# A decoder layer on one core: group 0's banded keys and values projected from unmodulated tokens, the adaLN shift added as a bias

## The chip, the cores and the metric

The kernel runs on one core of a Trainium2 chip. The metric is device time in microseconds (us) of one execution; the median over several executions counts. The engines of the core are TensorE (PE, with its weight loads listed as PEld), VectorE (DVE), ScalarE (ACT), GpSimd (POOL) and SyncE (SP). Each engine executes its own list of instructions strictly in that list's order; between engines, semaphores say when a tile is ready or free again.

## The reference, cut to what matters

One layer for S = 2048 tokens of width D = 1024. It begins with

```python
mod = silu(c) @ w_ada + b_ada                 # w_ada: 1024 x 3072
shift, scale, gate = split(mod, 3)
h = rms_norm(x, g_pre) * (1.0 + scale) + shift
proj = h @ w_in
qa, ka, va, fa, za, qb, kb, vb, zb = split(proj)
oa = forgetting_attention(qa, ka, va, fa + b_fgate) * silu(za)
ob = sliding_window_sink_attention(rope(qb), rope(kb), vb) * silu(zb)
y = concat(oa, ob) @ w_out
x = x + gate * rms_norm(y, g_post)
```

What the change touches is the way from x, `scale` and `shift` to h, and from h to `kb` (the keys of the sliding-window branch, 128 columns), `vb` (its values, 128 columns) and `fa` (the logits of the forget gates, 8 columns).

Written per column d of x, with xn the normalised x, G[d] = g_pre[d](1 + scale[d]), and shift[d]: h = xn G + shift, so h @ W = xn @ (G W) + shift @ W. The kernel before takes the left side for every token. The kernel after takes the right side for the first 512 tokens of kb, vb and fa.

## The kernel before, in words

**Groups and units.** The tokens stand in four groups of 512 (`ci` 0 to 3), each of four tiles `xt` of 128 tokens; the 1024 columns stand in eight slices of 128 (`KT`, index k). `hT[ci]` holds h transposed (columns on the partitions), as a high and a low float16 part. A weight is scaled by a power of two, made into a high part (`w_high`, ACT) and a low part (`w_low`, DVE), and a product is three float16 matmuls per slice: high x high, low x high, high x low. A unit of `kb` is one slice (three matmuls of 128x512), a unit of `vb` is four slices for 128 tokens (twelve matmuls of 128x136, values and forget gates together). `zb0` is a quarter of the weights of the banded branch's gate; its units look like those of `kb`.

**The start block.** It runs before the first unit and is written out by hand, engine by engine:

1. `c` is turned to columns, silu is taken. The positions are spread over 128 partitions by a matmul, and DVE makes the rotary angles from them (multiplied, reduced by 2 pi in six steps, clipped: tiles `ang`, `kh`, `kl`), ACT the sines.
2. The adaLN product: half 1 of `w_ada` is `scale`, half 0 is `shift`. Each half is eight tiles `wa` of 512 KB. Some are multiplied on PE (`ada_pe`, four float32 matmuls of 128x512 each), some are multiplied by silu(c) and added up on DVE (`ada_dve`, into `acc`), and `ada_sum` adds `acc` with a matmul against ones. `ada_col` picks the column form out of the sum (eight small DVE instructions).
3. Group 0: `squares` (ACT, a sum of squares per token tile), `root` (1/sqrt of the mean by a shift of the bits and three Newton steps, twelve instructions of 128x4: on DVE for group 0, on POOL for the others), `normal` (x times that root).
4. `pH`, a power of two that bounds h, and the factors `Gp` and `Shp` (G and shift, scaled by 2^14 / pH).
5. `turn`: four PE transposes per slice, then ACT applies `Gp` and `Shp` (Identity with scale and bias; the high part directly, the float32 `hf` beside it) and DVE takes the low part.

Group 1's squares, root and the normalisation of two of its tiles stand in this block too.

**The units and their slices.** After the start block a list `punits` runs in order: per group `kb` (8 units), `vb` (8 units), then some others; for group 0 that is `zb0` group 0 (8 units). Between them stand the transposes of the next group (`turn_x`, four of 128x128 per slice k, then ACT and DVE as in `turn`) at the places of the table `at_`. `at_slice(n, f)` puts an action at unit n (squares, root and normal of group ci + 2 in this manner), and `after(n, f)` puts the evacuation of a result one or more units behind the unit. The order on each engine is fixed by this program text; nothing is rearranged at run time.

**Queues.** SP's queue loads x and `w_ada`: x tiles 0 and 1 behind the scale half, x tiles 2 and 3 between tiles 1 and 2 of the shift half, x tiles 4 to 7 behind that. A transfer on it starts only when the one eight places ahead has landed. POOL's queue loads the weights of `kb`, `vb`.

**The end.** The output stage takes its own 1/sqrt with the same bit shift and Newton steps (`rsqrt_parts`, DVE), between the last product and the last store.

## Time and profile before

| | |
|---|---|
| median of 3 runs | 1151.11 us (1150.71 to 1152.66) |
| profiled execution: span from first to last instruction | 1149.5 us |
| profiled execution: mean granted TensorE clock | 0.995 of full |
| PE busy | 1117.5 us, 97% of the span |
| DVE, ACT, POOL busy | 930.4, 660.2, 211.1 us |
| DMA moved | 119.84 MB, mean 104 GB/s |

The span of the profiled execution lies 1.6 us below the median of the runs. "Busy" is the time in which an engine executed; matmuls are pipelined, so a busy PE is one that has a matmul under way, not one at its peak. The stretch that the change touches is the first 125 us and the last 10 us of the span.

### The profile page before, as it was taken

To read this page: it belongs to the slowest core of one execution; us is meant where nothing else is said; L and a number is where in the kernel's file an instruction comes from. 1 tells how busy PE (TensorE), PEld (TensorE's weight loads), DVE (VectorE), ACT (ScalarE), POOL (GpSimd) and SP (SyncE) were. 2 spreads that over 40 slices of the span, in tenths; PEclk is the share of its full clock that TensorE was granted. 3 is DMA by queue.
4 is the path that set the end of the run, shared out by engine and by line. 5 is a ranking of instruction groups with operands and counts; after the bars stand their busy time and mean duration, and the time that the engine had idled before them with its cause. 6 is when DMAs were issued, how large, how long until landed. Compare 5 with 4: busy or idle time off the path is not lost. (4 is left out here: it accounts for less than half of the span.)

```text
span 1149.5 us, 25258 instructions
## 1 busy us (share of the span) xinstructions
PE 1117.5 (97%) x9854; PEld 653.9 (57%) x9854; DVE 930.4 (81%) x2149; ACT 660.2 (57%) x1148; POOL 211.1 (18%) x328
## 2 busy tenths in 40 slices
PE   7899999999999999999999999999999999999997
PEld 3466545667755855555555555555555555544444
DVE  7878468968988568889888899888888888778885
ACT  3776245655555412676767667666776778634332
POOL 1222135645566420010010110001000000000000
PEclk8999999999999999999999999999999999999999
DMA  9934254423232232443244342213311336687643
GB/s 338 347 96 88 74 100 80 101 60 93 58 85 84 55 94 52 82 102 29 79 65 88 83 72 70 37 48 78 44 43 34 85 96 216 142 222 202 199 138 110
DMA packets 123134, 119.84 MB, mean 104 GB/s; under 512 B 64729, under 2 KB 100610, under 8 KB 123014
## 3 DMA queue, kind: packets, MB, share of 16 engines
q1 hardware_dynamic: 112046, 85.69, 27.3%
q0 software_dynamic: 10816, 32.50, 13.3%
q8 instruction: 77, 1.26, 0.6%
q14 instruction: 43, 0.35, 0.1%
q10 hardware_dynamic: 152, 0.04, 0.0%
HBM read 64.49 MB, written 25.18 MB: 78 GB/s over the span
## 5 line engine op out<-in xcount | busy, mean ns | idle before, releaser
L1367 ACT ACTIVATE p<-sta,lift,scl_qk 128x1024 f32<-128x1024 f32 (+2 forms) x160 | 171.9, 1075 | 131.0 <-PE sta L1361 82.0
L353 PE MATMUL bk<-hT,wh_qk 128*128 128x512 f16 x768 | 194.7, 378 | 0.0
L1374 DVE TENSOR_TENSOR pha<-p,pha 128x1024 f16<-128x1024 f32 (+2 forms) x160 | 169.1, 1057 | 0.2 <-ACT pha L1371 0.2
L1314 DVE TENSOR_REDUCE a_m<-bk 128x1 f32<-128x512 f32 x192 | 130.4, 686 | 45.5 <-PE bk L1311 44.5
L1589 PE MATMUL bk<-wohl,oz 128*128 128x512 f16 x744 | 163.7, 379 | 1.1 <-DVE oz L1538 0.7
L1371 ACT ACTIVATE pha<-p 128x1024 f16<-128x1024 f32 (+2 forms) x160 | 148.1, 926 | 5.9 <-PE poa L1387 1.2
L1589 PEld LDWEIGHTS <-oz 128*128 128x128 f16 x744 | 70.6, 98 | 84.6 <-DVE oz L1538 1.8
L1387 PE MATMUL poa<-vt,pha 128*128 128x65 f16 x1088 | 116.1, 192 | 1.4 <-DVE pha L1374 1.4
L1384 PE MATMUL poa<-vt,pha 128*128 128x65 f16 x1088 | 116.6, 193 | 0.8 <-DVE ona L1393 0.7
L1386 PE MATMUL poa<-vt,pha 128*128 128x64 f16 x1088 | 116.6, 194 | 0.0
L353 PEld LDWEIGHTS <-wh_qk 128*128 128x128 f16 x768 | 72.1, 97 | 74.5 <-issue 2.1
L1360 PE MATMUL sta<-T 128*128 128x512 f16 (+1 forms) x320 | 110.9, 346 | 2.9 <-ACT p L1367 2.8
L1311 PE MATMUL bk<-T 66*128 66x512 f16 (+2 forms) x320 | 109.7, 348 | 2.8 <-DVE a_m L1314 1.9
L1384 PEld LDWEIGHTS <-pha 128*128 128x128 f16 x1088 | 101.5, 96 | 15.5 <-DVE ona L1393 1.9
L1361 PE MATMUL sta<-T 69*128 69x512 f16 (+1 forms) x320 | 109.8, 348 | 0.0
L1386 PEld LDWEIGHTS <-pha 128*128 128x128 f16 x1088 | 100.9, 97 | 11.4
L1387 PEld LDWEIGHTS <-pha 128*128 128x128 f16 x1088 | 100.8, 99 | 1.8 <-DVE pha L1374 1.8
L353 PE MATMUL bk<-hT,wh_za 128*128 128x512 f16 x384 | 99.7, 378 | 0.0
L353 PE MATMUL bk<-hT,wh_zb 128*128 128x512 f16 x384 | 92.1, 379 | 0.5 <-ACT wh_zb L271 0.3
L371 PE MATMUL bk<-wh_va,hT 128*128 128x256 f16 x768 | 91.9, 273 | 0.0
L353 PE MATMUL bk<-hT,wh_qb 128*128 128x512 f16 x384 | 91.2, 379 | 0.0
L371 PEld LDWEIGHTS <-hT 128*128 128x128 f16 x768 | 73.3, 98 | 12.2 <-issue 2.1
(459 smaller groups left out, 1919.0 us busy)
## 6 DMA issues: line engine op xcount, KB each, us to landing
hT<-in_x_dram SPq DMA_DIRECT2D x20, 512.0 KB
wa<-in_w_ada_dram SPq DMA_DIRECT2D x16, 512.0 KB
z_d<-tz POOLq DMA_DIRECT2D x32, 256.0 KB, 2.9
T<-z_d SPq DMA_DIRECT2D x16, 512.0 KB
T<-stq SPq DMA_DIRECT2D x62, 128.0 KB
out_dram<-hT SPq DMA_DIRECT2D x15, 512.0 KB
xt<-in_x_dram SPq DMA_DIRECT2D x12, 512.0 KB
qs<-qf SPq DMA_DIRECT2D x80, 64.0 KB
```

Of the source, the lines that this page charges most:

```text
L353: PE.matmul(ps, whl[:, a, k, :], hT[ci][:, b, k, :], start=(k == 0 and n == 0), stop=(k == KT - 1 and n == 2))
L371: PE.matmul(ps[:, (u % 2) * 2 * P:(u % 2 + 1) * 2 * P], hT[ci][:, a, k, u * P:(u + 1) * P], wv[p][:, b, k, :], start=(k == 0 and n == 0), ...
L1314: V.tensor_reduce(m3[:, u, pc:pc + 1], mx[:, :w], axis=AX.X, op=ALU.max)
L1360: PE.matmul(self.st[:, o:o + w], T[:, 3, kb_], T[:, 1, qc], start=True, stop=False)
L1361: PE.matmul(self.st[:, o:o + w], T[0:XR, 2, kb_], T[0:XR, 0, qc], start=False, stop=not diag)
L1367: A.activation(self.p32[:, :self.w], self.st[:, :self.w], AF.Exp, scale=scl[f"qk{self.hd}"][:], bias=lift[:])
L1371: A.activation(self.ph[:, 0, :self.w], self.p32[:, :self.w], AF.Copy)
L1374: V.tensor_tensor(self.ph[:, 1, :self.w], self.p32[:, :self.w], self.ph[:, 0, :self.w], op=ALU.subtract)
L1384: PE.matmul(po[:, u, :], ph[:, 0, pq], vt[:, b, hd, 0:65], start=(self.first and n == 0 and u == 0), stop=False)
L1386: PE.matmul(po[:, u, 0:64], ph[:, 0, pq], vt[:, b, hd, 65:VW], start=False, stop=False)
L1387: PE.matmul(po[:, u, :], ph[:, 1, pq], vt[:, b, hd, 0:65], start=False, stop=(self.last and n == len(self.blocks) - 1))
L1589: PE.matmul(py, self.hl[:, i, k, :], w_slot(8 * j + k)[:, cc], start=(k == 0 and m_ == 0), stop=(k == KT - 1 and m_ == 2))
```

## The change

**Order of the start.** All four x tiles of group 0 are loaded between the two halves of `w_ada`. The `wa` tiles lie in the memory of `hT[1]` and `hT[2]`, which are not yet in use, so there are eight of them, each used for one tile of each half. On DVE the angles are split in parts and stand behind the copy of the columns `cols` and between the `ada_dve` steps of the scale half. Bounds are taken from maxima (`mx5`, `top`) with one transposition instead of a second matmul for the bound of h.

**Group 0.** x is only normalised, then transposed (`turn_plain`: ACT copies the high part, DVE subtracts the low one). The weights of `kb`, `vb`, `fa` are multiplied per row by `Gs` (G times a power of two) and split (`w2_high` 16 on ACT, `w2_low` 16 on DVE). The units of `kb` and `vb` for group 0 stand in the start block, among the matmuls of the shift half (`ada_pe` for tiles 0 to 2, `ada_dve` for tiles 3 to 7). Then comes `shift`: `ada_sum(0)` stands in the middle of the `vb` units, and the factors `Gp`, `Shp`, `Gx` behind it. shift @ W is made with small matmuls (`pb`; for `vb` from `shb`, `Shp` spread along the free axis by two POOL copies of 128x1024) and added when the results are evacuated (`bkb`, `bvb`).

**The plain weights.** For groups 1 to 3 `w_scale`, `w_high` and `w_low` of `kb` and `vb` are made as before, behind the factors of the shift half.

**Groups 1 and 2.** Squares, root and normal of group 1 stand behind that. Group 0's place in `punits` is sixteen empty units; group 1's transposes stand in a row between them. Squares, root and normal of group 2 stand among the units of group 1, not of group 0; those of group 3 remain there.

**Later modulation.** `remake(k)` modulates `hT[0]` slice by slice among group 1's units (two ACT and two DVE instructions of 128x512 for each of eight slices). The units of `zb0` for group 0 move to the list of `ci == 2`.

**1/sqrt.** All of them become a power of -0.5 on POOL, two instructions for a group, and in the output stage two POOL instructions and one on DVE. `gacc` takes a factor 32 in an instruction that was there.

The diff, cut to its core:

```diff
+    def remake(k):
+        hg = hst.tile([P, CH], F32, tag="hf", name="hg")
+        hi, lo = hT[0][:, 0, k, :], hT[0][:, 1, k, :]
+        A.activation(hg[:], lo, AF.Identity, scale=Gx[:, k:k + 1], bias=Shp[:, k:k + 1])
+        def high():
+            V.scalar_tensor_tensor(hg[:], hi, Gx[:, k:k + 1], hg[:], op0=ALU.mult, op1=ALU.add)
+            A.activation(hi, hg[:], AF.Copy)
+        after(1, high)
+        after(2, lambda: V.tensor_tensor(lo, hg[:], hi, op=ALU.subtract))
...
     def root(ci):
         ss, rst = rstd[ci]
-        rsqrt_mean(rst, ss[:], 4, G if ci else None)
+        f = 1.0 if ci else 2.0 ** -18
+        rv = sm(4, "rs_v")
+        G.tensor_scalar(rv[:], ss[:], f / D, f * EPS, op0=ALU.mult, op1=ALU.add)
+        G.tensor_tensor(rst[:], rv[:], mhalf[:].broadcast_to([P, 4]), op=ALU.pow)
...
         for k in (1, 3, 5, 7):
             ada_pe(1, k)
-        for k in (2, 4, 6):
-            ada_dve(1, k, k == 2)
-        for k in range(2):
-            load_ada(0, k)
-        for t in range(2, 4):
-            load_x(t)
-        for k in range(2, KT):
+        angle_a()
+        ada_dve(1, 2, True)
...
+        ada_dve(1, 6, False)
+        ada_sum(1, True)
...
+        ada_pe(0, 0, True)
+        turn_plain(0)
+        turn_plain(1)
+        ada_pe(0, 1)
+        for k in range(2, KT):
+            turn_plain(k)
+            ku[k - 2]()
+            if k == 4:
+                ada_pe(0, 2)
+                ada_dve(0, 3, True)
+            if k == 6:
+                ada_dve(0, 4, False)
+        for k in range(KT):
+            w2_high(k, P, VB)
+            w2_low(k, P, VB)
+            if k == 1:
+                ada_dve(0, 5, False)
+            if k == 5:
+                ada_dve(0, 6, False)
+        ku[6]()
+        ku[7]()
+        ada_dve(0, KT - 1, False, 2)
+        for n, u in enumerate(vu):
+            if n == 4:
+                ada_sum(0, True)
+            u()
...
+        w_scale("kb")
+        w_high("kb")
+        w_low("kb", 0, 1)
+        w_scale("vb")
+        w_high("vb")
+        w_low("vb", 0, 1)
...
+        squares(1)
+        root(1)
...
-        add("kb", kb_units(ci))
-        add("vb", vb_units(ci))
+        if ci == 0:
+            punits += [lambda: None for _ in range(16)]
+        else:
+            add("kb", kb_units(ci))
+            add("vb", vb_units(ci))
         if ci < 3:
-            add(*others[ci])
+            if ci:
+                add(*others[ci])
             if ci == 2:
+                add(*others[0])
...
+                for k in range(KT):
+                    at_slice(n0 + 20 + 3 * k, lambda k=k: remake(k))
...
-                    for _ in rsqrt_parts(self.rst, self.ss[:, 2:3], 1, self.more):
-                        pass
+                    V.tensor_tensor(self.more, self.ss[:, 2:3], self.more, op=ALU.add)
+                    G.tensor_tensor(self.rst[:], self.more, mhalf[:], op=ALU.pow)
```

Three places where the order of an engine moves. A row is: line, operation, output, inputs, shape, and how many alike stand in a row.

The first is DVE in the scale half, before (`ang`, `kh`, `kl` are the angles; `cols` is the copy of the columns that a PE transposition made; `acc1` collects the scale half, `wr_kv` holds the weights of `kb` and `vb`, whose maxima are taken):

```order
L583 SCALAR_TENSOR_TENSOR ang_222<-kl_224,ang_222 128x512
L585 TENSOR_SCALAR ang_222<-ang_222 128x512
L590 SCALAR_TENSOR_TENSOR kh_223<-ang_222 128x512
L591 TENSOR_SCALAR kh_223<-kh_223 128x512
L596 COPY cols_192<-bk2_138 128x32
L537 TENSOR_SCALAR acc1_207<-wa12_163,sil_126 128x1024
L539 SCALAR_TENSOR_TENSOR acc1_207<-wa14_167,sil_126,acc1_207 128x1024
L539 SCALAR_TENSOR_TENSOR acc1_207<-wa16_171,sil_126,acc1_207 128x1024
L619 TENSOR_REDUCE mx3_288<-wr_kv_183 128x1 x2
```

The same place after:

```order
L633 MEMSET zero_213 128x128
L644 COPY cols_194<-bk2_143 128x32
L648 TENSOR_REDUCE mx5_227<-cols_194 128x1 x3
L667 TENSOR_SCALAR ang_231<-bk1_142,colc_193 128x512
L668 TENSOR_SCALAR kl_233<-ang_231 128x512
L669 TENSOR_SCALAR kl_233<-kl_233 128x512
L670 TENSOR_SCALAR kh_232<-kl_233 128x512
L671 TENSOR_SCALAR kh_232<-kh_232 128x512
L672 TENSOR_TENSOR kl_233<-kl_233,kh_232 128x512
L612 TENSOR_SCALAR acc1_209<-hT1_108,sil_132 128x1024
L676 SCALAR_TENSOR_TENSOR ang_231<-kh_232,ang_231 128x512
```

The copy of `cols` stood behind all angles, and stands now ahead of the first. The multiplications into `acc1`, which stood behind the angles in a row, are now spread between them.

The second is ACT around the squares of group 1 (`junk`, with `hT3` as the memory of group 1's x tiles), before:

```order
L271 ACTIVATE wh_vb_343<-wr_kv_183,w_sw_338 128x1088
L433 ACTIVATE xt0_175<-xt0_175,rst_295 128x1024
L433 ACTIVATE xt1_177<-xt1_177,rst_295 128x1024
L433 ACTIVATE xt2_264<-xt2_264,rst_295 128x1024
L433 ACTIVATE xt3_266<-xt3_266,rst_295 128x1024
L421 ACTIVATE junk_409,ss_407<-hT3_110 128x1024
L421 ACTIVATE junk_411,ss_407<-hT3_110 128x1024
L421 ACTIVATE junk_413,ss_407<-hT3_110 128x1024
L447 ACTIVATE hT0_107<-px_383,Shp_115,Gp_114 128x512
L447 ACTIVATE hf_388<-px_383,Shp_115,Gp_114 128x512
L447 ACTIVATE hf_394<-px_389,Shp_115,Gp_114 128x512
L447 ACTIVATE hT0_107<-px_395,Shp_115,Gp_114 128x512
```

and after (`wh_x` are the weights scaled by G, `wh_kb` and `wh_vb` the plain ones, `qf` the evacuation of group 0's keys, `hT1` and `hf` the modulation of group 1):

```order
L763 ACTIVATE hT0_107<-px_431 128x512
L737 ACTIVATE wh_x_333<-wr_kv_185,Gs_331 128x136 x8
L275 ACTIVATE wh_kb_604<-wr_kv_185,w_sw_601 128x1024
L275 ACTIVATE wh_vb_614<-wr_kv_185,w_sw_611 128x1088
L425 ACTIVATE junk_675,ss_673<-hT3_110 128x1024
L425 ACTIVATE junk_677,ss_673<-hT3_110 128x1024
L425 ACTIVATE junk_679,ss_673<-hT3_110 128x1024
L928 ACTIVATE qf_739<-bk0_141,bkb_119,s0_kb_117 128x512
L425 ACTIVATE junk_681,ss_673<-hT3_110 128x1024
L532 ACTIVATE vb_735<-vt0_752 128x2x64 x2
L532 ACTIVATE vb_735<-vt0_754 128x2x64 x2
L452 ACTIVATE hT1_108<-px_776,Shp_115,Gp_114 128x512
```

Group 1's squares stood behind the normalisation of group 0 and ahead of its modulation. They stand now behind the two plain weights and just ahead of group 1's modulation.

The third is ACT in the units of group 1, where group 2 is modulated into `hT2`, before (`tz` is the gate `zb0` of group 0, `qf` and `stb` are the keys of group 1, `xt12` to `xt14` belong to group 3):

```order
L447 ACTIVATE hf_895<-px_890,Shp_115,Gp_114 128x512
L398 ACT_TABLE_LOAD
L398 ACTIVATE tz_900<-bk0_136,cz_zb0_768 128x512
L765 ACTIVATE qf_935<-bk1_137 128x512
L447 ACTIVATE hT2_109<-px_956,Shp_115,Gp_114 128x512
L447 ACTIVATE hf_961<-px_956,Shp_115,Gp_114 128x512
L447 ACTIVATE hf_995<-px_990,Shp_115,Gp_114 128x512
L819 ACTIVATE vb_568<-bk2_138 128x2x64 x2
L447 ACTIVATE hT2_109<-px_1025,Shp_115,Gp_114 128x512
L447 ACTIVATE hf_1030<-px_1025,Shp_115,Gp_114 128x512
L421 ACTIVATE junk_1040,ss_1038<-xt12_574 128x1024
L421 ACTIVATE junk_1067,ss_1038<-xt13_576 128x1024
```

and after (`xt8` to `xt11` are group 2's squares, `hg` is `remake`):

```order
L425 ACTIVATE junk_888,ss_886<-xt8_696 128x1024
L425 ACTIVATE junk_893,ss_886<-xt9_698 128x1024
L425 ACTIVATE junk_898,ss_886<-xt10_700 128x1024
L275 ACTIVATE wh_zb0_918<-wr_zb0_283,w_sw_915 128x1024
L425 ACTIVATE junk_920,ss_886<-xt11_702 128x1024
L930 ACTIVATE qf_925<-bk1_142 128x512
L507 ACTIVATE vb_735<-bk2_143 128x2x64 x2
L452 ACTIVATE hT2_109<-px_1009,Shp_115,Gp_114 128x512
L452 ACTIVATE hf_1014<-px_1009,Shp_115,Gp_114 128x512
L425 ACTIVATE junk_1050,ss_1048<-xt12_744 128x1024
L452 ACTIVATE hf_1057<-px_1052,Shp_115,Gp_114 128x512
L507 ACTIVATE vb_735<-bk0_141 128x2x64 x2
```

Group 2's squares stood further up, among the units of group 0. They stand now between the modulation of group 1 and that of group 2, with the weights of `zb0` among them; from the second slice of group 2 on, squares of group 3 and pieces of `remake` alternate with the modulation.

More of the change, by code (lines that the diff above doesn't have):

```diff
@@ L493, in hybrid_layer @@
             load_ada(1, k)
-        for t in range(2):
+        for t in range(4):
             load_x(t)
@@ L646, in hybrid_layer @@
-        ada_pe(0, 5)
-        ada_pe(0, 6)
-        root(0)
-        normal(0)
-        w_low("kb", 0, 1)
-        ada_dve(0, 4, False)
-        w_low("vb", 0, 1)
-        ada_dve(0, KT - 1, False, 2)
-        ada_sum(0, True)
-        turned = [turn(0, k) for k in range(4)]
-        squares(1, range(3))
+        gm = st.tile([P, 1], F32, name="gm")
+        V.tensor_scalar(gm[:], top1[:, 0:1], mr[:, 2:3], 1.0, op0=ALU.add, op1=ALU.add)
+        V.tensor_tensor(gm[:], gm[:], mr[:, 0:1], op=ALU.mult)
@@ L687, in hybrid_layer @@
-        V.tensor_reduce(mxs[:, 2:3], wq["zb0"][0][:], axis=AX.XY, op=ALU.max, apply_absolute_value=True)
-        V.tensor_scalar(dgz[:], ident[:], mxs[:, 2:3], None, op0=ALU.mult)
+        V.tensor_scalar(Gx[:], Gp[:], 2.0 ** -9, None, op0=ALU.mult)
+        sh2 = st.tile([P, KT, 2], F16, name="sh2")
+        V.tensor_copy(sh2[:, :, 0], Shp[:])
+        V.tensor_tensor(sh2[:, :, 1], Shp[:], sh2[:, :, 0], op=ALU.subtract)
+        shb = st.tile([P, 2, KT, P], F16, name="shb")
+        for b in range(2):
+            G.tensor_copy(shb[:, b], sh2[:, :, b].unsqueeze(2).broadcast_to([P, KT, P]))
@@ L1020, in z_all @@
     def z_all():
-        PE.matmul(bk[2][:, 0:P], ones[:], dgz[:], start=True, stop=True)
+        PE.matmul(bk[2][:, 0:P], ones[:], csum[:].rearrange("p h t -> p (h t)"), start=True, stop=True)
         V.tensor_reduce(mxs[:, 2:3], bk[2][:, 0:P], axis=AX.X, op=ALU.max)
@@ L1256, in gate_use @@
         else:
[L1257 removed]
+            V.scalar_tensor_tensor(gacc[:], gacc[:], 32.0, gw[k][:], op0=ALU.mult, op1=ALU.mult)
     def const_rows(n, eng):
```

328 lines of the change are left out of this document (205 added, 123 removed).

## The prediction

> **What bounds the kernel now.** I read the page's first part, then stretches of the span side by side, then PE's own instructions in the start. Columns of a stretch: its bounds and length, busy time (and instructions) of PE, PEld, DVE, ACT, POOL, PE's granted clock, DMA share, GB/s.
>
> ```profile
> span 1149.5 us, 25258 instructions
> PE 1117.5 (97%) x9854; PEld 653.9 (57%) x9854; DVE 930.4 (81%) x2149; ACT 660.2 (57%) x1148; POOL 211.1 (18%) x328
> ...
> 40.00:60.00 20.00, 15.84 (x146) 10.68 (x145) 16.97 (x45) 14.61 (x26) 6.89 (x13) 1.00 0.92 292
> 60.00:80.00 20.00, 18.87 (x152) 12.62 (x150) 17.54 (x35) 14.78 (x24) 7.08 (x14) 1.00 0.49 120
> 80.00:100.00 20.00, 20.00 (x195) 14.42 (x193) 14.53 (x34) 13.90 (x25) 6.17 (x15) 1.00 0.28 64
> 100.00:120.00 20.00, 20.00 (x118) 11.52 (x116) 14.62 (x33) 11.01 (x18) 2.18 (x4) 1.00 0.36 76
> ```
>
> PE is busy in 97% of the span and without a gap from 80 us on, so a unit that runs later by t in the start makes the end later by t; only idle time of PE before 80 us (4.2 us in 40 to 60, 1.1 in 60 to 80) can be won back. So I follow PE's list through the start: when does each piece begin, and which engine does it wait for?
>
> ```profile
> 9.54 0.31 PE L531 MATMUL bk<-ident,rows 32*128 32x32 f32 x1
> 15.12 8.41 PE L525 MATMUL pm<-wa,silb 128*128 128x512 f32 x12 [2.80 <-DMA wa<-in_w_ada_dram]
> 23.36 1.88 PE L525 MATMUL pm<-acc,ones 128*128 128x512 f32 x4
> 38.39 1.91 PE L441 MATMUL px<-ident,xt 128*128 128x128 f32 x16
> 58.38 0.49 PE L441 MATMUL px<-ident,hT 128*128 128x128 f32 x3
> 59.38 0.87 PE L811 MATMUL bk<-wh_vb,hT 128*128 128x136 f16 x12
> 75.31 0.87 PE L811 MATMUL bk<-wh_vb,hT 128*128 128x136 f16 x12
> 89.68 5.34 PE L353 MATMUL bk<-hT,wh_kb 128*128 128x512 f16 x24
> 94.86 5.84 PE L811 MATMUL bk<-wh_vb,hT 128*128 128x136 f16 x96
> ```
>
> Columns: start, time, engine, line, operation, output<-inputs, shape, count, and the idle time before with what ended it. The marks to compare with: group 0's transposes begin at 38.39, its last `vb` unit ends at 60.25 (59.38 + 0.87), group 1's transposes begin at 58.38, its `vb` at 75.31, group 2's `vb` at 94.86.
>
> **The change, part by part.** Each sum runs down the list of one engine.
>
> *1. The scale half is complete later, about +2 us.* DVE:
>
> ```profile
> 5.93 0.75 DVE L566 TENSOR_SCALAR ang<-bk,colc 128x512 f32<-128x512 f32 x1 [1.21 <-PE bk L513]
> 15.06 0.18 DVE L596 COPY cols<-bk 128x32 f32<-128x32 f32 x1
> 19.01 1.28 DVE L539 SCALAR_TENSOR_TENSOR acc<-wa,sil,acc 128x1024 f32<-128x1024 f32 x1 [1.26 <-DMA wa<-in_w_ada_dram]
> 20.21 2.40 DVE L619 TENSOR_REDUCE mx<-wr_kv 128x1 f32<-128x1024 f32 x2
> 24.42 0.29 DVE L548 SCALAR_TENSOR_TENSOR acc<-pm,ident 128x128 f32<-128x128 f32 x1 [1.80 <-PE pm L525]
> 24.64 0.29 DVE L548 SCALAR_TENSOR_TENSOR acc<-pm,ident 128x128 f32<-128x128 f32 x1
> 1133.24 0.15 DVE L101 TENSOR_SCALAR rs_v<-y_ss 128x1 f32<-128x1 f32 x1
> 1133.43 0.15 DVE L106 TENSOR_SCALAR rs_h<-rs_v 128x1 int32<-128x1 int32 x1
> ```
>
> The angles began at 5.93 and the copy behind them at 15.06: 9.13 us. Now the copy stands ahead, and it waits for the transposition that ends at 9.85 (9.54 + 0.31). From 9.85: copy and three small reductions (0.19 from start to start, as 1133.24 to 1133.43) 0.75, angles 9.13, three multiplications (0.70, 1.28, 1.28) 3.26, two maxima 2.40: `acc` is complete at 25.4, before at 20.3. PE was the later one before (its multiplications ended at 23.5), so the sum of the half begins at 25.4 instead of 23.36 and ends at 27.3 (1.88).
>
> *2. Group 0 is ready about 1.5 us earlier.* Behind that sum: one transposition, a small reduction and a small matmul about 0.8; `ada_col` with two maxima of 128x512 (taken as 0.69, the mean that the page gives for such a reduction, L1314) and eight picks at 0.22 (24.42 to 24.64) 3.1; ten small steps at 0.19 to `Gs` 1.9: 33.1. Eight `w2_low` of 128 columns at 0.22 and three normalisations at 0.70 (row below): 3.9. The first transposition is at about 36.9, against 38.39. Squares of group 0 (ACT, 1.27 each, behind x at about 25) and its root on POOL run beside this; ACT's `w2_high` pace DVE at equal price.
>
> ```profile
> L1314 DVE TENSOR_REDUCE a_m<-bk 128x1 f32<-128x512 f32 x192 | 130.4, 686 | 45.5 <-PE bk L1311 44.5
> 69.37 1.41 DVE L435 TENSOR_SCALAR xt<-xt,rst 128x1024 f32<-128x1024 f32 x2
> ```
>
> *3. Group 0's projection ends 1 us earlier.* PE from 36.9 in its order: eight slices of transposes (16 matmuls in 1.91, so 0.48 a slice) 3.8, six `kb` units (24 matmuls in 5.34, so 0.67 each) 4.0, two `ada_pe` at 1.88 3.8: the last slice's low part is there at about 48.7. Only then does DVE come to the `w2_low` of the values (8 x 0.22) and, between and behind them, to the last `ada_dve` steps (two at 1.28, one in two parts 1.3): `acc` of the shift half at about 54.5. The sum of that half ends at 56.8 (1.88, between `vb` units), and the four units behind it (96 matmuls in 5.84, so 0.73 each) at 59.6, against 60.25.
>
> *4. Group 1 begins 17 to 18 us later.* This is the term that decides. `shift` now ends at 56.8, where the kernel before had it at 38.6. Behind it in order: `ada_col` 3.1, some eleven small steps to `Shp` (60.5), three more to the plain weights; on ACT `w_high` of `kb` (1.13, row below), on DVE `w_low` (1.28), `w_scale` of `vb`, on ACT `w_high` of `vb` (1.13): about 66. ACT's next rows are the four squares of group 1. They need nothing of this, their x has landed by 41, and before they ran at 36.74; they are merely behind. Four at 1.27 and the wait for the fourth's sum: 71.3. POOL's two steps to the root 1.2 (bounds below), four normalisations 2.8 with the two larger steps of `csum` ahead of them on DVE: 76.1 for the first transpose, against 58.38: +17.7. PE has only the bias matmuls (40 small ones, about 2.5 us) between 59.6 and 76.1.
>
> ```profile
> 36.74 1.06 ACT L421 ACTIVATE junk<-hT 128x1024 bf16<-128x1024 f32 x1 [0.24 <-DMA hT<-in_x_dram]
> 38.03 1.06 ACT L421 ACTIVATE junk<-hT 128x1024 bf16<-128x1024 f32 x1
> 49.63 0.83 ACT L447 ACTIVATE hf<-bk,Shp,Gp 128x512 f32<-128x512 f32 x1
> 50.30 0.84 ACT L447 ACTIVATE hf<-px,Shp,Gp 128x512 f32<-128x512 f32 x1
> 59.38 1.13 ACT L271 ACTIVATE wh_zb<-wr_zb,w_sw 128x1024 f16<-128x1024 f32 x1
> 71.42 1.28 ACT L398 ACT_TABLE_LOAD   x1
> ```
>
> *5. `kb` of group 1.* ACT paces it: twelve modulations at 0.67 (49.63 to 50.30) are 8.0, with the keys' evacuation 8.6, then the last low part and its matmuls: `vb` of group 1 begins at about 88, against 75.31: +12.6. It is less than 17.7 because eight units of `zb0` that stood here (8 x 0.67 = 5.3) are owed now.
>
> *6. Group 2.* Behind the modulation of group 1 ACT has four squares (5.1) and one weight (1.04) before the root can begin, so it comes at 93.4 and the normalised tiles from 97.1; PE has run out of `vb` units at 91.4 (5.7 us idle). Then ACT must do, from 97.7, twelve modulations 8.0, four squares of group 3 5.1, four pieces of `remake` at 1.1, a table load 1.28 and three small evacuations 1.5: 20.3, with some 3 us of waits for DVE's half of each `remake`. `vb` of group 2 begins at about 122.6, against 94.86: +27.7. With the 5.3 us of `zb0` still owed: +33.
>
> *7. The end.* The bit shift and Newton steps run between the last sum and the last scaling:
>
> ```profile
> 1142.87 0.15 DVE L103 SCALAR_TENSOR_TENSOR rs_v<-y_ss,a_ri 128x1 f32<-128x1 f32 x1
> 1144.59 0.16 DVE L118 SCALAR_TENSOR_TENSOR y_rs<-rs_t,rs_y 128x1 f32<-128x1 f32 x1
> 1144.78 1.42 DVE L1618 SCALAR_TENSOR_TENSOR hT<-hT,y_rs 128x512 f32<-128x512 f32 x2
> ```
>
> 1.9 us of them shrink to one DVE step and one POOL step. No power stands in the trace of before. Its nearest rows are POOL's chain for the same root:
>
> ```profile
> 45.80 0.29 POOL L114 TENSOR_TENSOR rs_t<-rs_y 128x4 f32<-128x4 f32 x1 [4.78 <-DVE rs_y L107]
> ...
> 52.48 0.20 POOL L121 TENSOR_TENSOR rst<-rs_t,rs_y 128x4 f32<-128x4 f32 x1
> ```
>
> One step takes 0.2 at least and the twelve take 6.9. I take 0.7, the price of a middling single step, since it is one instruction; the ends stay for the range. So the end gains about 1.1.
>
> *8. PE's clock, +3.* Where PE ran dry at 12.3, the clock was down some 2 us later and up again some 6 us after the restart:
>
> ```profile
> 12.00:14.00 2.00, 0.32 (x1) 0.00 (x0) 1.86 (x5) 0.01 (x1) 0.00 (x0) 1.00 0.94 380
> 14.00:16.00 2.00, 0.88 (x1) 0.50 (x2) 1.87 (x4) 1.44 (x3) 0.00 (x0) 0.59 1.02 420
> 16.00:18.00 2.00, 2.00 (x4) 0.83 (x3) 1.28 (x1) 0.72 (x3) 0.00 (x0) 0.50 1.03 418
> 20.00:22.00 2.00, 2.00 (x4) 0.72 (x3) 2.00 (x3) 0.50 (x1) 0.00 (x0) 0.71 1.02 408
> ```
>
> Idle stretches of 3.7 us (33 to 36.9), 14 and 5.7 follow now, and six us at half clock behind each would cost up to 3 us of PE's time where PE is the pace, nothing where ACT is. Bounds 0 and +7; I take +3. [...]
>
> *At nothing:* the loads of `w_ada` into the memory of `hT` (the shift tiles land by about 36, DVE wants the last at 53); x tiles 2 and 3, now ahead of the shift half on SP's queue; x tiles 4 to 7, one place of eight further back, 20 us before they are used; the POOL copies for `shb` (2 of 128x1024, under POOL's wait for the root); the factor 32 in `gacc`. Without that cover each is 1 to 3 us. If group 1's wait were gone, the `remake` pieces and group 2's squares would be late next.
>
> **The sum.** +33 (wait of group 1, of group 2 and the owed units), -1.1, +3: +34.9 on the span of 1149.5, which lies 1.6 under the median of 1151.11. Forecast 1186.
>
> **The rivals.**
>
> *A: only group 1's wait counts.* If DVE's and ACT's pieces fit between, group 2 loses nothing more: +17.7, the end -1.1, clock 0 to +3, 1168 to 1171. For it speaks that ACT was busy 13.9 of 20 us there; against it that the squares of groups 2 and 3 and the `remake` stand in ACT's list between the very modulations that PE waits for.
>
> *B: the power is slow.* At 3 us it adds 2.3 to the root of group 1, of group 2 and to the end: 1193; at 6 us about 1202. For it: no row shows one. Against it: a single POOL step of 128x4 takes 0.2 to 0.83. [...]
>
> *C, the other side: faster.* Group 0 gains what it promises, 1 us at 59.6 and 1.1 at the end, and group 1 is not late. That holds only if its first transpose comes by about 58 to 60, and then the owed units fill PE's former idle time: about 1147. ACT has room between 50 and 60 for the squares. But they stand behind `w_high` of `vb`, which stands behind `shift`; `shift` would have to end some 16 us earlier than I reckon, at about 41, and the DVE list alone (low parts of all eight slices ahead of the last product) forbids that unless group 0's slices run far ahead of the pace of step 3.
>
> **How the numbers follow.** The forecast as summed 0.67 (its own range 1178 to 1194), A 0.15, B 0.10, C 0.04, the rest, mixtures of A and the forecast, 0.04. From 1164 to 1198 some 0.85 lies inside. 0.2% (2.3 us) is about what a measurement can tell here from no change: faster than that only C, 0.04; within it 0.02, a mixture of C and A; slower 0.94.
>
> **What would show it.** Right: PE idle or nearly so between about 60 and 76 us, the idle time ended by DVE's normalisation of `hT` tiles; ACT's squares of group 1 beginning at about 66, right behind `wh_vb`; a second gap of 5 us at about 92; `vb` of group 2 at about 122. Step 1: the sum of the scale half at 25.4 instead of 23.36. Step 7: the last scaling about 1 us closer to its sum. Wrong: squares of group 1 before 60, the shift half's sum before 50, or ACT with gaps while group 2 is modulated.

## The result, and the profile after

The changed kernel takes 1192.01 us (median of 4 runs, 1189.56 to 1192.75) against 1151.86 (4 runs, 1150.71 to 1152.66): a ratio of 1.0346 with a 95% interval of 1.0334 to 1.0359, slower by 3.5%. The forecast was 1186 in a range of 1164 to 1198. The profiled execution has a span of 1190.8 us, 41.3 more than before; the forecast was 34.9 more. Of the executions of all runs one, of `before_pow` below, was slow (1979.87 us at a mean granted clock of 0.615), and it is left out of the ratios and spreads.

The page of the changed kernel, its head, and PE's instructions at the marks of the prediction (columns as there):

```profile
span 1190.8 us, 25244 instructions
PE 1129.1 (95%) x9884; PEld 661.3 (56%) x9884; DVE 924.3 (78%) x2025; ACT 669.8 (56%) x1175; POOL 217.6 (18%) x334
...
24.90 1.98 PE L600 MATMUL pm<-acc,ones 128*128 128x512 f32 x4 [3.06 <-DVE acc L614]
34.11 0.48 PE L762 MATMUL px<-ident,xt 128*128 128x128 f32 x1 [1.65 <-DVE xt L754]
56.95 1.93 PE L600 MATMUL pm<-acc,ones 128*128 128x512 f32 x4
58.72 3.00 PE L499 MATMUL bk<-wh_x,hT 128*128 128x136 f16 x48
64.93 0.19 PE L827 MATMUL pb<-sh,wh_kb 128*128 128x2 f16 x1 [3.20 <-ACT wh_kb L275]
75.51 1.05 PE L446 MATMUL px<-ident,hT 128*128 128x128 f32 x2 [3.36 <-DVE hT L440]
89.85 3.71 PE L499 MATMUL bk<-wh_vb,hT 128*128 128x136 f16 x60
96.15 0.30 PE L446 MATMUL px<-ident,xt 128*128 128x128 f32 x1 [2.58 <-DVE xt L440]
116.21 2.17 PE L357 MATMUL bk<-hT,wh_kb 128*128 128x512 f16 x4 [3.03 <-DVE hT L456]
129.20 7.68 PE L499 MATMUL bk<-wh_vb,hT 128*128 128x136 f16 x96
```

The brackets tell the story. At these places the kernel before had no wait above 0.4 us; PE now waits for the plain weights (3.20), for the normalisation of group 1 (3.36), for that of group 2 (2.58) and for group 2's high parts (3.03). Mark by mark:

| mark (us) | before | forecast | after |
|---|---|---|---|
| sum of the scale half begins | 23.36 | 25.4 | 24.90 |
| group 0's first transpose | 38.39 | 36.9 | 34.11 |
| sum of the shift half begins | 36.57 | 54.9 | 56.95 |
| group 0's last `vb` unit ends | 60.25 | 59.6 | 61.72 |
| group 1's first transpose | 58.38 | 76.1 | 75.51 |
| group 1's `vb` begins | 75.31 | 88 | 89.85 |
| group 2's `vb` begins | 94.86 | 122.6 | 129.20 |

The 41.3 us come apart as follows: 34.3 at group 2's `vb` (129.20 - 94.86); 1.8 more because these 96 matmuls ran partly at half clock (7.68 us at a mean granted clock of 0.75, against 5.84 at 1.00); 5.2 for the eight `zb0` units of group 0 that were still owed; 1.1 back at the end; the other 1.1 in small waits later, which differ between executions. From 201 us on PE's busy time is that of the kernel before behind 160 (971.27 and 970.96): the work there is the same.

The stretches, in the same columns as before:

```profile
40.00:60.00 20.00, 17.32 (x128) 11.15 (x127) 13.73 (x30) 5.97 (x14) 0.00 (x0) 0.98 0.74 240
60.00:80.00 20.00, 8.68 (x82) 7.06 (x80) 14.89 (x57) 9.56 (x17) 4.23 (x5) 0.62 0.25 63
80.00:100.00 20.00, 14.93 (x119) 10.65 (x119) 15.53 (x33) 14.37 (x25) 1.38 (x2) 0.93 0.35 77
100.00:120.00 20.00, 16.22 (x99) 10.07 (x97) 10.60 (x19) 14.22 (x26) 2.43 (x4) 0.84 0.25 49
```

Against before, PE is busy for 1.5 us more in 40 to 60 and for 10.2 less in 60 to 80 (8.68 of 20 us). DVE is not the limit in 100 to 120 (10.60 us), although PE waits for it: it waits itself. Its list there, with the rows of SP's queue and ACT that belong to it:

```profile
93.57 0.57 ACT L930 ACTIVATE qf<-bk 128x512 f32<-128x512 f32 x1
99.47 0.59 SPq L485 DMA_DIRECT2D sinT<-sp__234  x1
100.16 2.44 SPq L932 DMA_DIRECT2D qs<-qf  x4
108.34 0.69 DVE L948 TENSOR_TENSOR qs<-qs,sinT 128x512 f32<-128x512 f32 x1 [6.70 <-DMA qs<-qf]
112.66 0.63 ACT L474 ACTIVATE hT<-hg 128x512 f16<-128x512 f32 x1 [2.24 <-DVE hg L473]
```

Group 1's keys are ready at 94.1. The copies that swap their halves (`qs`) can only be issued at 100.16, because sixteen copies of cosines and sines for groups 2 and 3 stand ahead of them on SP's queue. DVE reaches the instruction that needs `qs` at 101.6 and waits until 108.34; group 2's low parts stand behind it.

### The profile page after: what moved, and what is told of

Same layout as the page of the kernel before. It is cut to its first block, busy times and chain, and to the rows that moved or that the text cites. A ratio compares the mean times of both kernels' runs of the same rounds, so it can differ in the third digit from the quotient of the medians.

```text
span 1190.8 us, 25244 instructions
## 1 busy us (share of the span) xinstructions
PE 1129.1 (95%) x9884; PEld 661.3 (56%) x9884; DVE 924.3 (78%) x2025; ACT 669.8 (56%) x1175; POOL 217.6 (18%) x334
## 4 chain that ended last, share of the span: by engine, by line
PE 76%; DVE 15%; issue 3%; ACT 3%; DMA 2%; SPq 1%; POOL 0%; DVEq 0%; POOLq 0%; ACTq 0%
PE bk L357 28%; PE bk L1732 13%; PE bk L375 7%; PE sta L1505 4%; PE bk L1455 4%; PE sta L1504 4%; PE poa L1530 3%; PE poa L1531 3%; PE poa L1528 2%; DVE a_m L1458 1%; PE pss L1039 1%; PE pob L1096 1%; PE bk L499 1%; DVE pha L1518 1%; DMA qs<-qf 1%
```

## The experiments

Medians are set against the changed kernel's 1192.01, whose runs spread over 3.2 us; a difference under 2 us is therefore not told from none. The kernel before had medians of 1151.86, 1150.66, 1151.38 and 1151.40 beside them.

| run | median | against changed | ratio to before (95%) |
|---|---|---|---|
| squares_early | 1188.70 | -3.3 | 1.0324 (1.0306 to 1.0343) |
| spread_late | 1185.88 | -6.1 | 1.0300 (1.0283 to 1.0318) |
| remake_late | 1188.62 | -3.4 | 1.0324 (1.0308 to 1.0340) |
| shift_early | 1187.51 | -4.5 | 1.0321 (1.0298 to 1.0343) |
| all_four | 1178.67 | -13.3 | 1.0246 (1.0231 to 1.0261) |
| all_five | 1175.65 | -16.4 | 1.0212 (1.0189 to 1.0235) |
| all_six | 1170.78 | -21.2 | 1.0166 (1.0149 to 1.0184) |
| angles_first | 1190.02 | -2.0 | 1.0335 (1.0321 to 1.0348) |
| angles_whole | 1186.48 | -5.5 | 1.0304 (1.0287 to 1.0322) |
| warm | 1195.35 | +3.3 | 1.0379 (1.0365 to 1.0392) |
| before_pow | 1151.91 | | 1.0009 (0.9995 to 1.0023) |
| no_shift | 1147.03 | | 0.9959 (0.9943 to 0.9975) |

A single gain is best read at the stage that the edit changes as well. Far behind all edits, between 222 and 263 us, the profiled execution of the changed kernel has three waits for ACT of 2.8 us in all; the longest of them (columns: engine, output, line, what it waited for, us in total, times, longest):

```profile
PE pss L1039 <- ACT sm__2530 L1061: 1.8, 1, 1.8
```

The traces of the runs that change it in one place have 0.1 to 0.6 us there. So up to some 2.5 us of each gain in the table may not come of the edit; what makes these waits was not tested. At a mark that lies ahead of them, the begin of group 2's `vb` (129.20 in the changed kernel), the single edits give 1.6 us (squares_early), 4.0 (spread_late), 8.5 (remake_late), 4.0 (shift_early), 0.6 (angles_first) and 3.7 (angles_whole). The runs of squares_early (1187.1 to 1190.1), remake_late (up to 1189.7), shift_early (up to 1191.5) and angles_first (up to 1190.7) also overlap those of the changed kernel.

**Group 1's squares ahead of the plain weights (squares_early).**

```diff
         ada_dve(0, KT - 1, False, 2)
+        squares(1)
+        root(1)
         for n, u in enumerate(vu):
...
         w_high("kb")
+        normal(1, (0, 1))
         w_low("kb", 0, 1)
         w_scale("vb")
         w_high("vb")
+        normal(1, (2, 3))
         w_low("vb", 0, 1)
...
-        squares(1)
-        root(1)
...
-    for u in range(4):
-        at_slice(u, lambda u=u: normal(1, (u,)))
```

> Group 1's squares and root are put ahead of the plain weights (ACT idle at 51.8 to 63.7 us in the profile after), its normalisations between the steps of the plain weights. Theory 1 (the loss is an order: work that needs no shift stands behind shift): group 1's first transpose comes at about 72 instead of 75.5, its first modulation at about 73 instead of 78.7, and the end 5 to 6 us earlier, about 1186. Rival (group 2's own wait sets the time whatever group 1 does): the gap at 61.7 to 75.5 shrinks, the end moves by less than 2 us.

It gave 3.3 in the medians, between the two, but only 1.6 at group 2's `vb`, nearer to the rival. The squares moved into ACT's idle time (52.8 to 57.4) and PE's wait for the normalisation went. But PE's next matmuls came later, because DVE's normalisations now lay beside POOL's copies for `shb` (63.95 to 66.43) and took longer. DVE's two pairs, and PE's first wait behind them:

```profile
63.95 2.48 POOL L821 COPY shb<-sh 128x1024 f16<-128x1024 f16 x2 [0.33 <-DVE sh L817]
64.67 2.30 DVE L440 TENSOR_SCALAR hT<-hT,rst 128x1024 f32<-128x1024 f32 x2
68.72 1.41 DVE L440 TENSOR_SCALAR hT<-hT,rst 128x1024 f32<-128x1024 f32 x2
68.22 0.38 PE L833 MATMUL pb<-sh,wh_kb 128*128 128x1 f16 x8 [2.08 <-DVE w_p L89]
127.59 7.12 PE L499 MATMUL bk<-wh_vb,hT 128*128 128x136 f16 x96
```

The first pair took 1.15 us each beside POOL, the second 0.70 each. In this execution group 0 also began 1.4 us later, since the four matmuls of the sum ahead of it took 3.44 us instead of 1.98 (last section), of which 1.0 was left at the sum of the shift half (57.98 against 56.95). So of the 2 us by which the small matmuls come later (68.22, in the changed kernel 66.25) about half is the slower normalisation. Group 1's first transpose came at 73.92, its modulation at 77.1 instead of 78.7: the series behind shift holds it, not the squares alone.

**The copies of cosines behind group 1's keys (spread_late).**

```diff
-            at_slice((12, 22, 30)[ci], lambda ci=ci: spread(ci + 1))
+            at_slice((12, 36, 44)[ci], lambda ci=ci: spread(ci + 1))
```

> The cosines and sines of groups 2 and 3 are copied out after group 1's keys, not ahead of them on SP's queue (16 copies, 11 us of issuing from 89.1 to 100.1 in the profile after). Theory 2 (DVE's 6.7 us wait for the swapped keys of group 1, not ACT, makes group 2 later than predicted): that wait falls from 6.7 to about 1 us and the end comes 5 to 6 us earlier, about 1186. Rival (ACT's squares and later modulation of group 0 set the pace of group 2 anyway): the wait goes but the end moves by less than 2 us.

Theory 2 holds: 6.1 us, and the wait for `qs` is no longer among DVE's waits, which are now (engine, output, line, what it waited for, us in total, times, longest):

```profile
DVE hT L457 <- ACT hf L452: 2.8, 5, 1.1
DVE wh_zb L281 <- ACT wh_zb L275: 2.6, 1, 2.6
DVE hg L473 <- ACT hg L470: 2.1, 2, 1.1
```

Of the 6.1, 4.0 are there when group 2's `vb` begins (125.23 against 129.20). The rest lies in the late waits for ACT (2.8 us in the changed kernel, 0.1 here), and that these went because of the edit is not shown.

**The later modulation of group 0, later still (remake_late).**

```diff
-                    at_slice(n0 + 20 + 3 * k, lambda k=k: remake(k))
+                    at_slice(n0 + 40 + 2 * k, lambda k=k: remake(k))
```

> The eight pieces of the later modulation of group 0 are moved behind group 2's keys; nothing else. Theory 2 (the wait for the swapped keys sets group 2's pace): ACT's list is about 5 us shorter between group 2's modulations but DVE still waits until 108, so 2 to 4 us are gained, about 1189. Rival (ACT with these pieces is the pace): all of their ACT time and the waits for DVE between them goes, 6 to 8 us, about 1185.

The end came 3.4 us earlier, as theory 2 has it, but that total agrees by luck. The trace shows two effects: group 2's `vb` began at 120.71, 8.5 us earlier, as the rival has it for that stage, although DVE still waited 7.4 us for `qs`; and PE then had new waits for ACT, among group 3's transposes:

```profile
120.71 6.72 PE L499 MATMUL bk<-wh_vb,hT 128*128 128x136 f16 x96
141.25 0.66 PE L446 MATMUL px<-ident,xt 128*128 128x128 f32 x4 [2.78 <-ACT hf L452]
145.10 0.66 PE L446 MATMUL px<-ident,xt 128*128 128x128 f32 x4 [1.90 <-ACT hf L452]
```

So ACT's extra work (two instructions for each slice) costs PE in both places that were tried, each time among transposes; moving it moved 4.7 us of the wait.

**The shift half's products into DVE's idle time (shift_early).**

```diff
         for k in range(2, KT):
             turn_plain(k)
             ku[k - 2]()
+            if k in (2, 3):
+                ada_dve(0, k + 1, k == 2)
             if k == 4:
                 ada_pe(0, 2)
-                ada_dve(0, 3, True)
+                ada_dve(0, 5, False)
+            if k == 5:
+                ada_dve(0, 6, False)
             if k == 6:
-                ada_dve(0, 4, False)
+                ada_dve(0, KT - 1, False, 2)
...
         for n, u in enumerate(vu):
-            if n == 4:
+            if n == 0:
                 ada_sum(0, True)
```

> The products of the shift half on DVE stand among group 0's low parts, in its idle time, and the sum stands ahead of group 0's values instead of among them. Theory 1 (shift is late because of its place in DVE's list, not because of its fetch, which ends at about 36): the shift half's sum begins at about 51 instead of 57, the factors are there 4 to 5 us earlier, and the end comes 3 to 5 us earlier, about 1188. Rival (the products delay group 0's low parts by as much as they bring): within 1 us of the changed kernel.

Theory 1 holds. The sum began at 52.30 instead of 56.95, group 1's first transpose at 71.35 instead of 75.51, and the end came 4.5 us earlier. The fetch was not what made shift late.

**The four together, and group 2's squares as a fifth (all_four, all_five).** The fifth edit:

```diff
         for t in range(8, 12):
             load_x(t)
+        squares(2)
+        root(2)
...
-                    at_slice(n0 + 4 + u, lambda u=u: squares(2, (u,)))
...
-                at_slice(n0 + 8, lambda: root(2))
```

> The four edits together: squares of group 1 early, copies of cosines late, later modulation late, products of the shift half early. If each wait is its own (theory 1 and 2 both), their gains in the medians (3.3, 6.1, 3.4 and 4.5 us) nearly add: 1175 to 1179. If they hide one another, 1181 to 1186. Were the order of these four the whole of the loss, the time would be within 10 us of the kernel before; I expect that it is not: group 1 still waits for the sum of the shift half, its factors, the plain weights and the bias.

> The four edits together and, fifth, group 2's squares and root behind the plain weights in the start block instead of among group 1's units. Step 6 of the prediction (PE waits some 5 us for group 2's root, because its squares stand behind group 1's modulation on ACT): the gap at 86 to 92 us goes, 4 to 5 us less than with four edits: 1174. Rival (the squares push group 1's modulation back by as much): the same as with four, 1178.

Four edits gave 13.3 of the 17.3 us that they gave alone. At group 2's `vb` they add in full: it begins at 109.71, 19.5 us earlier, where the single edits give 18.1; 5.3 are lost again in waits for ACT among group 3's transposes. The fifth gave 3.0 more in the medians, but the runs overlap (1176.6 to 1182.1 and 1174.8 to 1178.1), so the trace has to show it: PE's wait for group 2's first tile went, as step 6 had it. The first row is that tile's transpose with four edits; then the first and the second tile's with five:

```profile
88.94 0.30 PE L446 MATMUL px<-ident,xt 128*128 128x128 f32 x1 [2.60 <-DVE xt L440]
```

```profile
88.05 0.30 PE L446 MATMUL px<-ident,xt 128*128 128x128 f32 x1
89.53 0.33 PE L446 MATMUL px<-ident,xt 128*128 128x128 f32 x1 [1.19 <-DVE xt L440]
```

Three short waits for the normalisation of the other tiles (1.19, 0.34 and 0.33 us) are left; they stood there with four edits too.

**The angles (angles_first, angles_whole).** The first run put six of the fifteen angle instructions ahead of the copy of the columns, not all as its expectation says (which counts eleven); the second put all of them there:

```diff
-        V.tensor_copy(cols[:], bk[2][:, 0:4 * KT])
...
+        angle_a()
+        for n in range(3):
+            angle_b(n)
+        angle_c()
+        V.tensor_copy(cols[:], bk[2][:, 0:4 * KT])
...
         for k in (1, 3, 5, 7):
             ada_pe(1, k)
-        angle_a()
         ada_dve(1, 2, True)
-        angle_b(0)
-        angle_b(1)
         ada_dve(1, 4, False)
-        angle_b(2)
-        angle_c()
```

> The angles stand on DVE ahead of the copy of the columns, in one piece, as in the kernel before; the rest is the changed kernel. Step 1 of the prediction: the sum of the scale half then begins at about 22 instead of 24.9 and group 0's transposes about 3 us earlier; if nothing of the fetch of the shift half stands in the way, the end comes 2 to 3 us earlier, 1189. Rival (the shift half's products set the pace from 45 us on, whenever group 0 begins): no change within 1 us.

> The run before this moved only the first six of the angles' instructions ahead of the copy of the columns, and DVE then waited 2.98 us for a tile of w_ada. Here all eleven stand ahead of it, as in the kernel before. Step 1 of the prediction: the sum of the scale half begins at about 22 instead of 24.9, group 0's transposes 2 to 3 us earlier, the end 2 to 3 us earlier, about 1189. Rival (the scale half is bound by its fetch, so that DVE waits for tiles instead): the sum stays at 24 or later, no change within 1 us.

With six, DVE only waited elsewhere, for the tile whose product stands next, and the sum began at 24.64. With all fifteen there is work to do until that tile lands; the sum began at 21.58 and group 0's transposes at 30.69, 3.4 us earlier. The two rows, first that of six, then that of fifteen:

```profile
13.37 0.75 DVE L612 TENSOR_SCALAR acc<-hT,sil 128x1024 f32<-128x1024 f32 x1 [2.98 <-DMA hT<-in_w_ada_dram]
```

```profile
21.58 1.88 PE L600 MATMUL pm<-acc,ones 128*128 128x512 f32 x4
```

The end came 5.5 us earlier, more than the 2 to 3 expected: PE did not run dry ahead of this sum, and the 3.4 us of group 0 are there in full at group 2's `vb` (125.53, 3.7 earlier). The rest of the 5.5 is not seen in the stage.

**All six (all_six).**

> The five edits and all angles ahead of the copy of the columns. If the sixth brings what the whole angles bring alone: 2 to 3 us less than with five, 1171. Theory 4 (what is left is the design itself: group 1 cannot begin before the sum of the shift half, the factors, the plain weights and the bias, all in series, while PE has nothing else): still 15 us or more slower than the kernel before, first transposes of group 1 at 65 or later, against 58.4. Rival (only the order was wrong): within 5 us of the kernel before.

The sixth edit gave 4.9 us. The result, 1170.78, is still 19 us over the kernel before, and group 1's first transpose comes at 66.02. What PE does there, in series:

```profile
54.81 1.94 PE L499 MATMUL bk<-wh_x,hT 128*128 128x136 f16 x30
58.04 0.18 PE L828 MATMUL pb<-sh,wh_kb 128*128 128x2 f16 x1 [1.29 <-ACT wh_kb L275]
60.31 0.38 PE L830 MATMUL pb<-sh,wh_kb 128*128 128x1 f16 x8 [2.09 <-DVE w_p L89]
62.18 0.39 PE L835 MATMUL pb<-wh_vb,shb 128*128 128x136 f16 x2 [1.31 <-ACT wh_vb L275]
63.57 2.65 PE L835 MATMUL pb<-wh_vb,shb 128*128 128x136 f16 x22 [1.00 <-DVE wh_vb L281]
66.02 1.91 PE L446 MATMUL px<-ident,hT 128*128 128x128 f32 x8
```

This fits theory 4 as far as group 1 goes, but the series accounts for less than half of what is left. Of the 20.5 us between the profiled spans (1170.0 and 1149.5), 9.0 are there when group 2's `vb` begins (103.88 against 94.86). Another 5.2 are the `zb0` units that are owed, 4.0 are waits of PE for ACT among group 3's transposes, and some 3.4 are an estimate of what half clock costs there (the mean granted clock of 0.83 in 120 to 140 is as much as 6.8 us at 0.50); the end gains 1.1. So the rest is mostly what was moved behind. The run doesn't show that no other order would do better; none was found that beats the kernel before.

**What there was to win (no_shift).** The kernel before without the loads, products and sum of the shift half, whose product is taken as zero:

```diff
-        ada_pe(0, 0, True)
-        ada_pe(0, 1)
-        ada_dve(0, 2, True)
...
-        ada_sum(0, True)
...
-        ada_col(0, shf0)
+        V.memset(shf0[:], 0.0)
```

> The kernel before without the shift half: its eight tiles are not loaded, not multiplied and not summed, and the product is taken as zero (the bias part of shift stays). It gives the most that hiding the shift's fetch can bring, since here nothing of it is left. PE loses six blocks of four float32 matmuls (6 x 1.8 = 10.8 us), which the changed kernel still has to do. Theory 5 (there was next to no wait to fill: PE was busy with these blocks from 25 to 38 us): the gain is 8 to 11 us, 1140 to 1143, so no more than the work itself. Rival (PE waited for the fetch, and the change's cover is worth having): a gain of 14 us or more.

It gains 4.4 us (0.41%), less even than the 8 to 11 of theory 5. PE's waits from 20 to 60 us, first of the kernel before, then of this one:

```profile
PE bk L525 <- DMA wa<-in_w_ada_dram: 1.7, 2, 1.2
PE bk L353 <- DVE hT L452: 1.2, 4, 0.3
```

```profile
PE px L441 <- ACT xt L433: 6.8, 4, 5.1
PE bk L624 <- DVE dg L623: 1.4, 1, 1.4
```

The kernel before waits 1.7 us for tiles of `w_ada` in these 40 us. With the shift half gone PE waits 6.8 us for the normalised x in its place: the root and the weights stand ahead of it on DVE and ACT. So most of the freed time became another wait, and in this order 4 us is all that could come of hiding the whole shift half.

**The powers alone (before_pow).** In the kernel before, `root` and the output stage are taken from the changed one, with the factor 32.

> The kernel before with the change's powers alone: all roots by two POOL instructions, in the output stage one on DVE and one on POOL, the factor 32 in the gate. Step 7 of the prediction: the stretch from the last sum to the last scaling shrinks by about 1 us (the changed kernel's own trace has 0.83 there, the kernel before 1.9) and nothing else moves, since the roots of the start are hidden: 1149.6 to 1150.0 against 1150.7. Rival (POOL's power in the start delays group 0's normalisation): same or slower by up to 1 us.

The end is as expected; the first row is the last sum, the last the scaling, 0.82 us apart where it was 1.91:

```profile
1145.04 0.15 DVE L1573 TENSOR_TENSOR a_ri<-y_ss,a_ri 128x1 f32<-128x1 f32 x1
1145.86 1.42 DVE L1622 SCALAR_TENSOR_TENSOR hT<-hT,y_rs 128x512 f32<-128x512 f32 x2 [0.68 <-POOL y_rs L1574]
```

The time is not: 1151.91, with runs spread from 1149.4 to 1157.1 where the kernel before has 1150.1 to 1152.8. In the profiled execution ACT waited 1.46 and 0.90 us for x tiles of group 2 between 54 and 60 us, and group 1's `vb` began at 77.54 instead of 75.31. Three matmuls of 128x512 took 1.49 us at 64.21 there and three at 66.29 took 0.81, and the kernel before has a granted clock of 1.00 throughout 60 to 80 us; this is a part of it. The rival's reason, a later normalisation of group 0, is not seen: group 0's first transpose came at 38.01 (before 38.39). Why the x tiles came later is not settled.

**PE kept busy in its gaps (warm).** Transposes of the identity, of which nothing is read:

```diff
+        warm(bk[0][:, 256:384], 9)
         ada_pe(0, 0, True)
+        warm(bk[0][:, 256:384], 14)
         turn_plain(0)
...
+        warm(pb[0][:, 256:384], 24)
         PE.matmul(pb[0][:, 0:2], wq["kb"][:, 0, 0, :], sh2[:, 0, :], start=True, stop=False)
...
+                for n in range(1, 8):
+                    at_slice(n0 + n, warm_x)
```

> The changed kernel with idle PE transposes of the identity put into its gaps (9 and 14 at 28 to 34 us, 24 and 30 around the bias, 12 ahead of seven of group 2's key units); nothing is read of them. [...] Rival (half clock only where PE waits anyway): the clock stays up and the time is the same within 1 us.

A gain of 2 to 4 us was expected of it, with the granted clock at 1.0 in these stretches. It was 3.3 us slower, since the added transposes waited for buffers themselves (5.51 us for ACT at group 2's keys) and held PE's list. The total therefore decides nothing. Two stretches of it do:

```profile
76.00:80.00 4.00, 3.10 (x27) 2.68 (x26) 4.00 (x13) 1.51 (x5) 0.00 (x0) 1.00 0.46 107
...
134.39 5.84 PE L499 MATMUL bk<-wh_vb,hT 128*128 128x136 f16 x96
```

The mean clock in 62 to 76 was 0.76 (0.60 in the changed kernel), and in 76 to 80 it was 1.00 (0.50). Group 1 took as long from the sum of the shift half to its `vb` (57.76 to 90.51, 32.75 us) as with the low clock (56.95 to 89.85, 32.90). But group 2's `vb`, where PE is the pace, took 5.84 instead of 7.68. In these two stretches half clock cost time only where PE itself was the pace; the added transposes stood in the first of them, so its two lengths are not of one and the same list.

## Why the prediction was right, and where its sizes were off

- **Steps 1 and 2** held. The sum at 24.90 (25.4 forecast), 1.54 later than before; the first whole slice of transposes at about 37 (36.9), though the first transpose itself came at 34.11, since PE began with the first normalised tile and then waited. The reason holds too: with all angles ahead of the copy the sum begins at 21.58.
- **Step 3** was 2.1 us too good: `vb` of group 0 ended at 61.72. PE ran the first part of this piece at half clock (0.51 granted in 36 to 41 us; one `ada_pe` took 3.40 instead of 1.88), and the values' weights on DVE held two of its units by 0.94 and 1.13 us. So group 0 won nothing, it lost 1.5.
- **Step 4**, the deciding one, has the right mechanism, with the squares at 67.97 behind `wh_vb` and the gap ended by DVE's normalisation. That the time agrees to 0.6 us (75.51) is in part luck: the step puts the first transpose behind all four normalisations, which end at 78.18, 2.1 later than its 76.1, as the sum of the shift half began 2.1 later (56.95 against 54.9); but PE began with the first tile. Its 60.5 for `Shp` is also added up wrong: 59.9 and eleven steps at 0.19 are 62.0, and the trace has 62.56. What it did not see is that the squares alone are not the hold: moved away, they give 3.3 us in the medians and 1.6 at group 2's `vb`, since the bias and the plain weights run in series there.
- **Step 5** held (89.85 against 88).
- **Step 6** is the term that was mis-sized: group 2's `vb` came 34.3 us late, not 27.7. Of these 6.6 us 1.9 are there at group 1's `vb`, and 4.0 go when the wait for `qs` is taken away (spread_late; 6.1 in the medians); 0.7 is not assigned. The step reckoned ACT's list and left out SP's: in the kernel before DVE waits 2.5 us for `qs` at 85.06, and there the copies of cosines were out when the keys were ready, at 76.1; with keys 18 us later in the same order of copies these are still being issued, and the wait is 6.7. PE's gap for group 2's root was 4.4 in all, where the step had 5.7.
- **Step 7** held: 0.83 us in place of 1.91. The power took 0.56 (128x1) and 1.05 (128x4); 0.7 was taken.
- **Step 8** was about the right size: 1.8 at group 2's `vb` and some 1.5 at group 0, of which it is not shown what was left at the end. The 2 us and the 6 us that it read off one fall and one rise of the clock did not hold for the others: see the last section.
- **Costs taken as nothing:** the loads, x tiles and `gacc` cost nothing that the trace shows. POOL's copies did not delay what waits for them, but in squares_early, where two normalisations of DVE lie beside them, these took 1.15 us each instead of 0.70.
- **Rivals.** A fell: group 2 lost 20 us more than group 1's 14.5. B fell: the powers of 128x4 took 1.01 to 1.05 us in the changed kernel and at most 1.37 in before_pow, and no run shows one of 3 or 6. C failed at the point that it named: shift ended at 58.9, not 41.

## What to carry to other kernels

Before hiding a fetch, read how long the critical engine waits for it: here 1.7 us in a view of waits, and leaving the whole half out gained 4.4. A step that moves others behind a late value has to be priced by everything that stands behind it in the list of each engine, the DMA queue's too, and what is owed later is still owed. When a stage moves, re-place the transfers whose order was fitted to the old one.

## What the runs showed of the hardware that was not expected

**The clock fell at no fixed time behind PE's last work.** In the changed kernel the granted clock changes within these stretches (last columns: clock, DMA share, GB/s):

```profile
30.00:31.00 1.00, 0.68 (x2) 0.40 (x2) 0.94 (x11) 0.00 (x0) 0.00 (x0) 0.81 1.03 410
40.00:42.00 2.00, 2.00 (x9) 0.92 (x8) 0.00 (x0) 0.30 (x1) 0.00 (x0) 0.78 1.02 162
64.00:66.00 2.00, 0.19 (x1) 0.10 (x1) 1.10 (x1) 0.87 (x1) 0.94 (x1) 0.69 0.61 205
80.00:82.00 2.00, 2.00 (x12) 2.00 (x12) 1.75 (x4) 1.98 (x4) 0.00 (x0) 0.54 0.15 34
98.00:100.00 2.00, 1.37 (x9) 1.12 (x10) 2.00 (x6) 0.53 (x1) 0.00 (x0) 0.72 0.43 98
102.00:104.00 2.00, 2.00 (x22) 1.68 (x21) 0.00 (x0) 1.23 (x4) 0.00 (x0) 0.92 0.41 95
114.00:116.00 2.00, 0.00 (x0) 0.00 (x0) 0.95 (x3) 1.85 (x5) 1.23 (x2) 0.99 0.64 138
132.00:134.00 2.00, 2.00 (x29) 2.00 (x27) 2.00 (x4) 0.62 (x2) 0.00 (x0) 0.74 0.07 21
```

Taking one switch in each between 1.0 and 0.5, an estimate from these rows puts the falls at 30.62, 64.76, 98.88 and 115.96 and the rises at 40.88, 81.8, 102.3 and 133.04. The prediction read "some 2 us" off one fall, in the kernel before, which came 2.0 us behind PE's last work. Of the four falls here, those at 64.76 and 115.96 came 3.0 and 2.8 us behind it. That at 98.88 came among the transposes of 96.15 to 98.96, between which PE waited up to 1.19 us. That at 30.62 came when PE, behind waits of 1.05 and 0.32 us, had been at work again since 30.49. And two waits as long, of 2.77 and 3.06 us ahead of 14.73 and 24.90, passed without a fall: the granted clock was 1.00 from 8 to 30 us. The prediction's "some 6 us" from PE's restart to the rise were, counted from the end of PE's last wait, 4.4 here (36.49 to 40.88), 3.6 (78.23 to 81.8), 3.3 (98.96 to 102.3) and 5.4 (127.67 to 133.04). What makes the clock fall and rise is not shown by these runs.

One list also ran at different speeds in two executions: with squares_early the four matmuls of the sum of the scale half took 3.44 us, in the changed kernel 1.98 at a granted clock of 1.00, with the same list up to there; four such matmuls at 37.82 took 3.40 in the changed kernel, at a mean granted clock of 0.55. In this sum alone the two executions differ by 1.5 us, half of the spread of the changed kernel's runs.

**DVE's normalisations took longer beside POOL's copies.** Two of them beside POOL's copies took 2.30 us, two without 1.41 (squares_early). POOL's two copies took 2.48 us beside them, and 2.02 in the changed kernel. What makes them longer is not shown.

**POOL's powers of 128x4 took 1.01 to 1.37 us**, where the prediction took 0.7. In the changed kernel the first took 1.05 us and began 0.08 us behind the instruction before it; the later ones took 1.01 to 1.04. In `before_pow` the first took 1.37 us and the second 1.20.
